# Gram products of two head pairs in one block, and the recurrence's first sums directly behind the solve

## The chip, the cores and the metric

The kernel runs on one core of a Trainium2 chip. The metric is the device time of one execution in microseconds, as the median of several runs; lower is better.

## What is computed

The reference is a trunk of two layers on a sequence of 512 tokens with 1024 channels. Each layer normalizes its input, projects it with one wide matrix, runs three mixers side by side on the columns (an RWKV-7 recurrence, a chunked retention, a gated spatial mixing), merges them through sigmoid gates, and adds a gated MLP with a short convolution. Cut to its frame:

```python
for l in range(DEPTH):
    h = rmsnorm(x, norm1_g[l])
    p = h @ w_in[l]
    p_rw, p_ret, p_sg, gate_logits = jnp.split(p, in_cuts, axis=-1)
    y_rw = rwkv7_branch(p_rw, ...)          # 8 heads of 64 channels
    y_ret, y_sg = retention_branch(p_ret, cos, sin), sgu_branch(p_sg, ...)
    gates = jax.nn.sigmoid(gate_logits.reshape(B, S, N_BRANCH, D_MODEL))
    x = x + jnp.sum(gates * proj, axis=2) @ w_out[l]
    x = x + conv_ffn(rmsnorm(x, norm2_g[l]), ...)
return rmsnorm(x, final_g)
```

The change lies in the RWKV-7 branch, whose core is a recurrence over tokens:

```python
sa = jnp.einsum('bhvk,bhk->bhv', state, -kk_t)
state = state * w_t[:, :, None, :] + sa[..., None] * (kk_t * a_t)[:, :, None, :] + v_t[..., None] * k_t[:, :, None, :]
y = jnp.einsum('bhvk,bhk->bhv', state, r_t)
```

## The kernel before

All data are 32-bit floats. A large product is made of three matrix products of rounded halves (high x low, high x high, low x high; `mm3`, line 157), each 128x128 by 128x512. Weights come by DMA through the queue of SyncE, and ScalarE (line 140) and VectorE (line 141) split each block of 512 columns into its high and low half.

The recurrence is not run token by token. The 512 tokens are cut into 8 chunks of 64, and the 8 heads stand in 4 pairs `m`, one head on each half of the 128 partitions. The branch goes through these steps:

- Projections. `cols3(m)` computes the k, r and v columns of pair m (`col`, 24 dense products each), `col(13)` the columns of the output gate.
- `prep(m)` computes decay factors and the scaled operands `x` and `bk` on ScalarE and VectorE, from two small projections (lines 565 and 566). Then come its **Gram products** (lines 603 and 606): for each of two groups of four chunks, 16 products of 64x64 by 64x128 go into two PSUM tiles, `pB` and `pK`. ScalarE copies the tiles to `GB` and `Y` (lines 607 and 608), and POOL masks their upper triangles (lines 611 and 612).
- `bonus(m)` sums r times k over the channels of a head by two dense products with a block of ones (lines 620 and 621) and multiplies the sum with v.
- `vturn` and `bturn` transpose v and `bk` by way of DRAM; their DMAs stand in the queue of SyncE.
- `solve` inverts the 64x64 unit triangular matrix of each of the 64 head-chunks. Copies on ScalarE and POOL (lines 801 and 803) gather the 32x32 diagonal blocks, VectorE transposes them (line 813) and inverts them in 31 serial steps (lines 820 and 822), and after line 826 two rounds of 32x32 products join the halves (lines 841 and 850), each followed by copies out of PSUM (lines 845 and 854).
- The recurrence over the 8 chunks (products all on line 696) alternates with copies on VectorE and ScalarE. Its first products are the sums `Q` of chunk 0, from `Y` and the transposed v.

Where PE would stand still it works on **fillers**: projections that the branch doesn't need, the gates above all (`gates`, 24 column blocks of 24 products; one step of the generator, a fill, is 12 products). Before the change 36 fills stand between the last `prep` and the first 32x32 products, two between the rounds, one more and then one more ahead of `Q`, and one between the steps of each chunk.

What sets the order: the program is written as one stream of instructions, and a scheduler orders each engine's instructions ahead of time by data dependence, free buffers, program order as a priority and a simulated timeline. An instruction given to `keep_in_program_order` (`po` in the code, or `pin` in a fill) is ordered behind the instruction that the program wrote last for its engine; others may be taken between, and instructions without it may move ahead when they are ready earlier. Each engine then runs its list strictly in order.

PSUM has two pools of four tiles of 128x512: `acc` for the large products and `sm` for the small ones (`pB`, `pK`, the sums of `bonus`, the solve's tiles, `Q` and `P1`).

Of the kernel before, what the change touches and what calls it, by code (L numbers as in the profile page):

```python
# [21 lines left out]
RWC, RETC, SGC = 1792, 1536, 1024  # L22
NU, NR, NFP = 31, 16, 39
FIRST = (12, 4, 0, 8)
FILL = (36, 2, 1)
KEPT = 6
PRE = {(0, "f", 2): 0, (0, "f", 4): 1, (0, "f", 6): 2, (0, "f", 8): 3, (0, "d", 0): 4, (0, "d", 1): 5, (0, "d", 2): 6, (0, "d", 3): 7,
       (0, "d", 4): 8, (0, "d", 5): 9, (0, "d", 6): 10}
# [24 lines left out]
class Emit:  # L53
# [440 lines left out]
    def rwkv(self, l, nst):  # L494
        nc, V, A, a = self.nc, self.nc.vector, self.nc.scalar, self.a
        T, P = nc.tensor, nc.gpsimd
# [3 lines left out]
        po = self.tc.keep_in_program_order if l == 0 else lambda i: i  # L500
# [9 lines left out]
        n2, pr, sw = self.small((128, 4, 8), "n2"), self.small((128, 4, 16), "pr"), self.small((128, 4, 8), "sw")  # L510
# [11 lines left out]
        def col(m):  # L522
            ps = ready.pop(m) if m in ready else self.colF(l, m)
            p = self.r(n="rwp")
            V.tensor_tensor(p, ps, self.rsF, op=MUL)  # L525
# [7 lines left out]
        for i in range(2):  # L533
            x = self.u(n="wax")
# [23 lines left out]
        def prep(m):  # L558
# [3 lines left out]
            ms = slice(m * 128, m * 128 + 128)  # L562
# [4 lines left out]
            x, y = [self.rw((128, 8, 128), n, 4) for n in ("X", "Y")]  # L567
            bk = self.rw((128, 8, 2, 64), "bk", 4)
# [26 lines left out]
            V.tensor_tensor(bk[:, :, 1, :], q8(kp), q8(Eout), op=MUL)  # L595
            V.transpose(tha, ksq)
            V.tensor_reduce(pr[:, m], tha.rearrange("p (j r) -> p j r", r=32), axis=AX.X, op=ADD)
            for g in range(2):
                pB, pK = [self.sm((128, 4, 128)) for _ in range(2)]
                for j in range(4):  # L600
                    c = 4 * g + j
                    for h in range(2):
                        i = T.matmul(pK[hv[1 - h], j, :], bk[hv[h], c, 1, :], x[hv[h], c, :], start=True, stop=True)  # L603
                        if c or h:
                            po(i)
                        po(T.matmul(pB[hv[h], j, :], bk[hv[h], c, 0, :], x[hv[h], c, :], start=True, stop=True))
                A.copy(GB[:, 8 * m + 4 * g:8 * m + 4 * g + 4, :], pB)
                A.copy(y[:, 4 * g:4 * g + 4, :], pK)
            for h in range(2):
                yr, gr = y[hv[h]].rearrange("p c (a t) -> p c a t", a=2), GB[hv[h], 8 * m:8 * m + 8, 64:128]  # L610
                P.affine_select(yr, yr, [[0, 8], [1, 2], [1, 64]], ALU.is_ge, 0.0, base=-1, channel_multiplier=-1)
                P.affine_select(gr, gr, [[0, 8], [1, 64]], ALU.is_ge, 0.0, base=0, channel_multiplier=-1)
            X.append(x); Y.append(y); BK.append(bk)

        def bonus(m):
            kp, r, v = kc[m], rc[m], Vf[m]
            V.scalar_tensor_tensor(kp, r, self.p("rk", m), kp, op0=MUL, op1=MUL)
            kh, kl = self.split(kp, self.r)
            pbn = self.sm()
            po(T.matmul(pbn, self.bonesR, kl, start=True, stop=False))  # L620
# [15 lines left out]
        prep(1)  # L636
        cols3(3)
        bonus(1)
        prep(2)
        gd = col(13)  # L640
        bonus(2)
        prep(3)
        bonus(3)
        A.activation(gd, gd, AF.Tanh, scale=0.5)
        V.tensor_scalar(gd, gd, 0.5, 0.5, op0=MUL, op1=ADD)
# [24 lines left out]
        vop = lambda R, m, c: Vf[m][R].rearrange("p (e c d) -> p e c d", e=2, d=32)[:, :, c, :]  # L670
# [8 lines left out]
        n2 = n2.rearrange("p m c -> p (m c)")  # L679
# [5 lines left out]
            for m in range(4):  # L685
                bturn(m, 0)

        self.solve(GB, n2, turns)

        yT, mh = [], [(m, h) for m in range(4) for h in range(2)]

        def mm(o, l, r, start=False):
            po(T.matmul(o, l, r, start=start, stop=True, skip_group_check=True))  # L696

        while back:
            po(A.copy(*back.pop(0)))
        self.fill(1, True)  # L700
        self.fill(FILL[2], True)
        Q = self.sm((128, 2, 4, 64))
        for m, h in mh:
            mm(Q[hv[h], 1, m, :], Y[m][hv[1 - h], 0, 0:64], vop(hv[1 - h], m, 0), m == 0)
        for c in range(8):
            if c % 2 == 0:
                y = self.r(n="y")
# [77 lines left out]
            self.yrw.append(self.split(t, self.f))  # L785
            yield

    def solve(self, G, n2, then):


        V, A, T = self.nc.vector, self.nc.scalar, self.nc.tensor
# [56 lines left out]
        for g, i in [(g, i) for g in range(2) for i in range(16)]:  # L848
            for h in range(2):
                po(T.matmul(pt[g][h][(lo, hi)[i % 2][h], i, :], zs[g][hi[h], i, :], TT[hi[h], 16 * g + i, :], start=True, stop=True))  # L850
# [631 lines left out]
```

## Time and profile before

| what | value |
|---|---|
| median of 3 runs | 1690.54 us (1690.29 to 1692.25) |
| span of the profiled execution | 1688.8 us; no other time of that execution is given |
| PE (TensorE) busy | 1680.2 us, 99% |
| VectorE, ScalarE, POOL busy | 1217.9, 793.7, 261.3 us |
| granted TensorE clock | 1.000 over the span |
| Gram products, layers 0 and 1 | from 64.86 to 124.56 and from 898.33 to 975.40 us |
| solve's first product | at 197.59 and 1041.62 us |

A row of the timeline gives the start in microseconds from the beginning of the span, the duration, the engine, the line of the kernel, what is written and read, shapes and a count. Dense products overlap, so PE's progress is read from the distance of starts. Each of the small 32-bit products stands in the profile as two rows. A wait is written as the engine, line and tile that waited, the releaser behind an arrow, and the idle time.

### The profile page before, as it was taken

Reading aid. Unit: us, or ns where it says so; the run is one execution under the profiler, and the core shown is the slowest. Engines: PE = TensorE matmul, PEld = TensorE weight load, DVE = VectorE, ACT = ScalarE, POOL = GpSimd, SP = SyncE. Lnnn points to the kernel's source line nnn. Section 1 sums busy time; section 2 is a strip of 40 time slices with the busy share of each in tenths; the row PEclk is TensorE's granted clock in tenths of the full one; section 3 lists DMA queues with packets and bytes.
Section 4 is the critical chain, followed back from the end, with each engine's and each line's share of the span. In section 5 each row is a group of like instructions: output and inputs, shape, how many; then the busy total and the mean of one; then the engine's idle time right before and its main releaser. Section 6 shows DMA issues by size and latency. Waiting matters only on the chain.

```text
span 1688.8 us, 27952 instructions
## 1 busy us (share of the span) xinstructions
PE 1680.2 (99%) x10247; PEld 1381.5 (82%) x10247; DVE 1217.9 (72%) x2115; ACT 793.7 (47%) x1365; POOL 261.3 (15%) x376
## 2 busy tenths in 40 slices
PE   9999999999999999999999999999999999999998
PEld 7888877888888888888888888778888888888887
DVE  7887746578669877655568888465786688887877
ACT  6563433554255444433346544335542544444565
POOL 1121000312301200003321210003122012220000
PEclk9999999999999999999999999999999999999999
DMA  5236563634544533247743366536344434443775
GB/s 183 88 109 199 176 187 95 184 122 134 191 144 148 195 122 97 63 146 261 252 145 99 94 207 184 174 101 188 118 137 163 154 96 144 142 141 110 244 248 177
DMA packets 143385, 260.01 MB, mean 154 GB/s; under 512 B 19440, under 2 KB 35440, under 8 KB 143248
## 3 DMA queue, kind: packets, MB, share of 16 engines
q1 hardware_dynamic: 117056, 188.41, 35.9%
q0 software_dynamic: 17552, 54.15, 9.8%
q10 hardware_dynamic: 8640, 15.67, 2.6%
q8 instruction: 80, 1.31, 0.3%
q14 instruction: 57, 0.47, 0.1%
HBM read 212.94 MB, written 45.22 MB: 153 GB/s over the span
## 4 chain that ended last, share of the span: by engine, by line
PE 97%; DVE 1%; DMA 1%; issue 0%; ACT 0%; SPq 0%; ACTq 0%; DVEq 0%
PE acc L157 88%; PE sm L157 3%; PE sm L696 2%; PE sm L948 1%; PE sm L603 1%; PE sm L1059 0%; DMA wr<-wall 0%; DMA tr<-bkT 0%; DVE wl L141 0%; PE acc L359 0%; PE sm L566 0%; PE sm L565 0%; PE sm L1006 0%; PE sm L850 0%; PE acc L319 0%
## 5 line engine op out<-in xcount | busy, mean ns | idle before, releaser
L157 PE MATMUL acc<-lo,sh 128*128 128x512 f32 x1108 | 432.0, 390 | 0.0
L157 PE MATMUL acc<-hi,sh 128*128 128x512 f32 x1108 | 431.4, 389 | 0.0
L157 PE MATMUL acc<-hi,sl 128*128 128x512 f32 x1108 | 424.6, 389 | 0.0
L140 ACT CAST sh<-wr 128x512 fp32r<-128x512 f32 (+1 forms) x375 | 226.8, 614 | 309.1 <-PE acc L157 165.6
L141 DVE TENSOR_TENSOR sl<-wr,sh 128x512 fp32r<-128x512 f32 (+1 forms) x375 | 252.0, 680 | 94.9 <-ACT sh L140 78.9
L141 DVE TENSOR_TENSOR wl<-wr,wh 128x512 fp32r<-128x512 f32 x238 | 169.0, 713 | 139.4 <-ACT wh L140 133.6
L140 ACT CAST wh<-wr 128x512 fp32r<-128x512 f32 x238 | 146.8, 619 | 242.8 <-PE acc L157 154.6
L157 PEld LDWEIGHTS acc<-lo,sh 128*128 128x128 f32 x1108 | 208.0, 188 | 43.8 <-issue 0.3
L157 PEld LDWEIGHTS acc<-hi,sl 128*128 128x128 f32 x1108 | 208.0, 188 | 43.1 <-issue 0.2
L157 PEld LDWEIGHTS acc<-hi,sh 128*128 128x128 f32 x1108 | 208.0, 188 | 43.0
L157 PE MATMUL acc<-lo,wh 128*128 128x512 f32 x584 | 230.0, 394 | 0.4 <-DVE rwp L525 0.4
L157 PE MATMUL acc<-hi,wl 128*128 128x512 f32 x584 | 228.3, 391 | 0.1
L157 PE MATMUL acc<-hi,wh 128*128 128x512 f32 x584 | 227.6, 390 | 0.0
L1125 ACT ACTIVATE cv<-fu,pc 128x512 f32<-128x512 f32 x88 | 71.7, 816 | 138.4 <-DVE fu L1123 138.4
L157 PEld LDWEIGHTS acc<-hi,wl 128*128 128x128 f32 x584 | 109.6, 188 | 24.6 <-issue 0.9
L157 PEld LDWEIGHTS acc<-lo,wh 128*128 128x128 f32 x584 | 109.6, 188 | 24.2 <-DVE rwp L525 0.8
L157 PEld LDWEIGHTS acc<-hi,wh 128*128 128x128 f32 x584 | 109.7, 188 | 22.3 <-issue 0.2
L157 PE MATMUL acc<-ah,sh 128*128 128x512 f32 x352 | 108.4, 389 | 0.0
L1126 DVE SCALAR_TENSOR_TENSOR cv<-fu,pc,cv 128x511 f32<-128x511 f32 x88 | 65.8, 749 | 34.5 <-ACT cv L1125 34.4
L157 PE MATMUL acc<-wl,hi 128*128 128x512 f32 x212 | 85.7, 404 | 0.0
L1123 DVE TENSOR_TENSOR fu<-acc,rsF 128x512 f32<-128x512 f32 x88 | 60.3, 685 | 30.8 <-PE acc L157 29.8
L157 PE MATMUL acc<-wh,hi 128*128 128x512 f32 x212 | 82.5, 389 | 0.0
(368 smaller groups left out, 2447.5 us busy)
## 6 DMA issues: line engine op xcount, KB each, us to landing
wr<-wall SPq DMA_DIRECT2D x480, 256.0 KB, 2.9
gd<-gth ACTq DMA_DIRECT2D x48, 256.0 KB, 3.4
gth<-gd POOLq DMA_DIRECT2D x48, 256.0 KB, 3.7
pre<-wdt POOLq DMA_DIRECT2D x44, 256.0 KB, 6.1
ts<-pre POOLq DMA_DIRECT2D x44, 256.0 KB, 2.8
wr<-ts SPq DMA_DIRECT2D x44, 256.0 KB, 4.1
wr<-wdn SPq DMA_DIRECT2D x40, 256.0 KB, 4.3
wr<-wdt SPq DMA_DIRECT2D x33, 256.0 KB, 4.1
```

Source lines behind the costliest of these rows:

```text
L140: self.kept(self.nc.scalar.copy(hi[:, :n], raw[:, :n]))
L141: self.kept(self.nc.vector.tensor_tensor(lo[:, :n], raw[:, :n], hi[:, :n], op=SUB))
L157: i = self.nc.tensor.matmul(*x, **y, **kw)
L603: i = T.matmul(pK[hv[1 - h], j, :], bk[hv[h], c, 1, :], x[hv[h], c, :], start=True, stop=True)
L696: po(T.matmul(o, l, r, start=start, stop=True, skip_group_check=True))
L948: po(T.matmul(o, lhsT, rhs, start=start, stop=stop, skip_group_check=True))
L1123: V.tensor_tensor(u, ps, self.rsF, op=MUL)
L1125: A.activation(t, u, AF.Identity, scale=self.p("cw2", j), bias=self.p("cb", j))
L1126: V.scalar_tensor_tensor(t[:, 1:], u[:, :511], self.p("cw1", j), t[:, 1:], op0=MUL, op1=ADD)
```

## The change

`prep(m)` ends before its Gram products. They move to a new function `gram(ms)`, which writes them for two pairs, four groups one behind the other, with all products in program order. The two PSUM tiles of the third group are taken from the pool `acc`; those of the other three come from `sm`. The masks of POOL for both pairs follow behind the products of both.

The calls become: projections of all pairs and of the output gate ahead of `prep(2)`; `gram((1, 0))` behind `prep(2)`; 6 fills; `bonus(2)` and `prep(3)`; 6 fills; `gram((3, 2))`; `bonus(3)`. The fills between this point and the solve's first products go from 36 to 24, so their sum stays.

The sums `Q` of chunk 0 become a function `begin`, which `solve` calls between its second round of products and the copies of their result. `Q` now takes a tile of `acc`. The two fills that stood ahead of the sums now follow them.

```diff
-FILL = (36, 2, 1)
+FILL = (24, 2, 1)
+GRAM = (6, 6)
...
-            for g in range(2):
-                pB, pK = [self.sm((128, 4, 128)) for _ in range(2)]
+            X.append(x); Y.append(y); BK.append(bk)
+
+        def gram(ms):
+
+            for m, g in [(m, g) for m in ms for g in range(2)]:
+                x, y, bk = X[m], Y[m], BK[m]
+                pB, pK = [(self.acc if (m, g) == (ms[1], 0) else self.sm)((128, 4, 128)) for _ in range(2)]
                 for j in range(4):
                     c = 4 * g + j
                     for h in range(2):
-                        i = T.matmul(pK[hv[1 - h], j, :], bk[hv[h], c, 1, :], x[hv[h], c, :], start=True, stop=True)
-                        if c or h:
-                            po(i)
+                        po(T.matmul(pK[hv[1 - h], j, :], bk[hv[h], c, 1, :], x[hv[h], c, :], start=True, stop=True))
                         po(T.matmul(pB[hv[h], j, :], bk[hv[h], c, 0, :], x[hv[h], c, :], start=True, stop=True))
                 A.copy(GB[:, 8 * m + 4 * g:8 * m + 4 * g + 4, :], pB)
                 A.copy(y[:, 4 * g:4 * g + 4, :], pK)
-            for h in range(2):
+            for m, h in [(m, h) for m in ms for h in range(2)]:
...
         bonus(1)
+        gd = col(13)
         prep(2)
-        gd = col(13)
+        gram((1, 0))
+        self.pool = None
+        self.fill(GRAM[0])
         bonus(2)
         prep(3)
+        self.fill(GRAM[1])
+        gram((3, 2))
         bonus(3)
...
-        self.solve(GB, n2, turns)
+        def begin():
+
+            q = self.acc((128, 2, 4, 64))
+            for m, h in mh:
+                mm(q[hv[h], 1, m, :], Y[m][hv[1 - h], 0, 0:64], vop(hv[1 - h], m, 0), m == 0)
+            return q
+
+        Q = self.solve(GB, n2, turns, begin)
         while back:
             po(A.copy(*back.pop(0)))
         self.fill(1, True)
         self.fill(FILL[2], True)
-        Q = self.sm((128, 2, 4, 64))
-        for m, h in mh:
-            mm(Q[hv[h], 1, m, :], Y[m][hv[1 - h], 0, 0:64], vop(hv[1 - h], m, 0), m == 0)
...
                 po(T.matmul(pt[g][h][(lo, hi)[i % 2][h], i, :], zs[g][hi[h], i, :], TT[hi[h], 16 * g + i, :], start=True, stop=True))
+        q = begin()
         for g in range(2):
             for h in range(2):
                 for e in range(2):
                     (V.tensor_copy if h else A.copy)(G[lo[h], 16 * g + e:16 * g + 16:2, 32:64], pt[g][h][(lo, hi)[e][h], e::2])
+        return q
```

More of the change, by code (lines that the diff above doesn't have):

```diff
@@ L608, in prep @@
                 A.copy(y[:, 4 * g:4 * g + 4, :], pK)
-            for h in range(2):
-                yr, gr = y[hv[h]].rearrange("p c (a t) -> p c a t", a=2), GB[hv[h], 8 * m:8 * m + 8, 64:128]
+            for m, h in [(m, h) for m in ms for h in range(2)]:
+                yr, gr = Y[m][hv[h]].rearrange("p c (a t) -> p c a t", a=2), GB[hv[h], 8 * m:8 * m + 8, 64:128]
                 P.affine_select(yr, yr, [[0, 8], [1, 2], [1, 64]], ALU.is_ge, 0.0, base=-1, channel_multiplier=-1)
                 P.affine_select(gr, gr, [[0, 8], [1, 64]], ALU.is_ge, 0.0, base=0, channel_multiplier=-1)
-            X.append(x); Y.append(y); BK.append(bk)
         def bonus(m):
@@ L786, in rwkv_out, with solve @@
             yield
-    def solve(self, G, n2, then):
+    def solve(self, G, n2, then, begin):
         V, A, T = self.nc.vector, self.nc.scalar, self.nc.tensor
```

## The prediction

> **What bounds the kernel now.** I read the page first: the busy line and the chain that ended last.
>
> ```profile
> span 1688.8 us, 27952 instructions
> PE 1680.2 (99%) x10247; PEld 1381.5 (82%) x10247; DVE 1217.9 (72%) x2115; ACT 793.7 (47%) x1365; POOL 261.3 (15%) x376
> PE 97%; DVE 1%; DMA 1%; issue 0%; ACT 0%; SPq 0%; ACTq 0%; DVEq 0%
> ```
>
> PE is never without work, so a time is what PE issues plus what it waits. Next the list of waits of PE, all of it:
>
> ```profile
> PE acc L359 <- DVE rst L356: 1.5, 1, 1.5
> PE sm L620 <- ACT Y L608: 0.5, 1, 0.5
> PE sm L696 <- DVE s L756: 0.4, 2, 0.2
> PE acc L157 <- DVE rwp L525: 0.4, 1, 0.4
> ```
>
> That is 2.8 us, 1.5 of it at the very start. No wait stands at the Gram products (L603, L606) or at the solve (L841, L850). What is left to gain at these places is what PE loses when it goes from dense products to small ones and back, inside "busy". The chain in order of time shows dense stretches of three lengths (start, us, what):
>
> ```profile
> 8.44 13.60 PE acc L157 x60
> 198.92 5.67 PE acc L157 x24
> 212.25 2.95 PE acc L157 x12
> ```
>
> 60 in 13.60 us are 0.2267 us each. 24 of them should take 5.44 and 12 of them 2.72; both stretches take 0.23 more, whatever their length. The timeline of PE over the first Gram block of layer 0 shows where (start, duration; a duration is a product's latency, so I use differences of starts):
>
> ```profile
> 64.54 0.39 PE L157 MATMUL acc<-lo,wh 128*128 128x512 f32 x1
> 64.86 0.32 PE L603 MATMUL sm<-X,bk 64*64 64x128 f32 x1
> ...
> 65.02 0.27 PE L603 MATMUL sm<-X,bk 64*64 64x128 f32 x1
> ...
> 66.55 0.27 PE L603 MATMUL sm<-X,bk 64*64 64x128 f32 x1
> ...
> 66.77 0.50 PE L157 MATMUL acc<-hi,wh 128*128 128x512 f32 x1
> 67.11 0.40 PE L157 MATMUL acc<-hi,wl 128*128 128x512 f32 x1
> ...
> 67.58 0.40 PE L157 MATMUL acc<-hi,wh 128*128 128x512 f32 x1
> 68.43 0.50 PE L620 MATMUL sm<-lo,bonesR 128*128 128x512 f32 x1 [0.45 <-ACT Y L608]
> ```
>
> The 64 rows of a block are 32 products, two rows each, and start four at a time. From 65.02 to 66.55 fourteen fours pass, 0.109 us each; sixteen should take 1.75. The block takes 66.77 - 64.86 = 1.91, so 0.16 more. The way in is 0.32 instead of 0.227 (0.09 more), and the three dense steps after it take 0.81 instead of 0.68 (0.13 more). **One excursion from dense work to small work and back costs 0.38 us**, beside the small products themselves. The dense side of it, 0.09 + 0.13, is the 0.23 of the stretches above.
>
> **The change part by part.** No product is added or taken away: 432 fill products a layer stay 432 (36 fills of 12; after it 6 + 6 + 24), and the vector, scalar and POOL work of prep and solve keeps its instructions. What changes is the number of excursions, and who waits.
>
> *Gram in two blocks a layer instead of four.* Two excursions less a layer, four in the program: 4 x 0.38 = **-1.5 us**. Nothing hides it, since it lies on PE.
>
> *The first sums behind the solve's second product.* Before, 24 fill products separate the two:
>
> ```profile
> 204.52 1.46 PE L850 MATMUL sm<-cs,zs 32*32 32x32 f32 x128
> ...
> 211.57 0.68 PE L696 MATMUL sm<-Vt,Y 64*64 64x64 f32 x16
> 212.18 0.50 PE L157 MATMUL acc<-lo,wh 128*128 128x512 f32 x1
> ```
>
> Joined, the dense side's 0.23 is gone. But the products here go from tiles of 32x32 to tiles of 64x64, and no row of this trace shows that step. At best it costs nothing, and the narrow side's 0.16 is saved too (0.39 a layer); at worst it costs as much as the dense side (0 a layer). I take 0.2, in the middle, because every change of shape that has a row here costs something: **-0.4 us** for two layers, bounds 0 and -0.8. The Trainium skill (TensorEngine Tiling (Array Packing), Key Properties) says that changing the tiling mode, not just the tile, drains the engine; a 32x32 to 64x64 step is such a change. By that rule the join keeps a drain, and the sum would be at the 0 end, 0.4 us later than mine; the rows above agree with it as far as they go (dense to 64x64 is paid for both ways). The sums come out in a slot of the other PSUM pool and are held until the copy of L719; the fills need one slot of four in turn, so three serve them. What the sums no longer cover, the copies of the solve's result, still has three fills ahead of the first product that needs it: 36 x 0.2267 = 8.2 us against 24 before and 12 behind the sums, the same.
>
> *A wait that loses its cause.* The row of 68.43 above is the bonus product of pair 0: it needs a PSUM slot which the Gram copies on ACT hold. From 67.58 to 68.43 are 0.85 instead of 0.23, and the waits' view names it. After the change pair 0's and pair 1's bonus come ahead of any Gram product. **-0.6 us**, bounds 0 (it comes back at pair 3's bonus, which stands directly behind the second block) and -0.6.
>
> *A wait that gets a cause.* A merged block has four groups of two PSUM tiles. Three take slots of the small pool, which has four, and one takes the other pool's; so the fourth group needs the slots of the first, and starts at 3 x 0.875 = 2.63 us into the block (a group is eight fours of 0.109). They are free when ACT has made two copies. In layer 0's last block and in layer 1's first block (starts on PE, then ACT):
>
> ```profile
> 122.65 0.32 PE L603 MATMUL sm<-X,bk 64*64 64x128 f32 x1
> 123.81 0.59 ACT L608 COPY Y<-sm 128x512 f32<-128x512 f32 x1 [1.44 <-PE sm L606]
> 124.29 0.59 ACT L607 COPY GB<-sm 128x512 f32<-128x512 f32 x1
> ```
> ```profile
> 898.33 0.29 PE L603 MATMUL sm<-X,bk 64*64 64x128 f32 x1
> 904.15 0.62 ACT L140 CAST sh<-wr 128x512 fp32r<-128x512 f32 x1 [5.25 <-DMA wr<-wall]
> 906.80 0.58 ACT L607 COPY GB<-sm 128x512 f32<-128x512 f32 x1
> ```
>
> The first has its second copy done 2.23 us into the block (124.88): no wait, 0.4 to spare. In the second ACT sits in its order behind a cast whose weights are late, and is done at 9.05: PE would stand 6.4 us, and all dense work with it. Bounds 0 and 6.4 a block. The new blocks stand where the projections are over and fills run, like the first row, so I take 0.1 a block: **+0.4 us** over four. The Trainium skill (the same page, PSUM Bottleneck) says that tiling speeds up TensorE but not the emptying of PSUM; the copies, 0.48 us apart, against a group of two tiles in 0.875 bear it out. By that rule alone a block would go at ACT's pace, 4 x 0.96 instead of 4 x 0.875, and four blocks would cost 1.4 us instead of my 0.4: the first rival below.
>
> *The solve's cover.* The solve's serial chain (POOL copies, DVE steps) runs under the fills between the last Gram product and L841, and the products behind it are pinned, so lateness there is PE idle, one for one. Rows of POOL, DVE and PE:
>
> ```profile
> 125.44 2.37 POOL L611 TENSOR_SCALAR_AFFINE_SELECT Y<-Y 64x1024 f32<-64x1024 f32 x2 [14.26 <-ACT Y L608]
> 127.87 1.71 POOL L612 TENSOR_SCALAR_AFFINE_SELECT GB<-GB 64x512 f32<-64x512 f32 x2
> 129.53 2.60 POOL L803 COPY cs<-GB 32x1024 f32<-32x1024 f32 x2
> ```
> ```profile
> 136.78 0.69 DVE L141 TENSOR_TENSOR wl<-wr,wh 128x512 fp32r<-128x512 f32 x1 [3.75 <-ACT wh L140]
> ...
> 138.01 2.06 DVE L813 STREAM_TRANSPOSE cs<-cs 128x1024 f32<-128x1024 f32 x1
> ...
> 185.65 2.31 DVE L826 STREAM_TRANSPOSE cs<-cs 128x512 f32<-128x512 f32 x2
> ```
> ```profile
> 124.56 0.50 PE L157 MATMUL acc<-hi,wl 128*128 128x512 f32 x1
> ...
> 197.59 1.34 PE L841 MATMUL sm<-cs,GB 32*32 32x32 f32 x128
> ```
> ```profile
> 1034.02 2.27 DVE L826 STREAM_TRANSPOSE cs<-cs 128x512 f32<-128x512 f32 x2
> ```
> ```profile
> 975.40 0.50 PE L157 MATMUL acc<-hi,wl 128*128 128x512 f32 x1
> ...
> 1041.62 1.34 PE L841 MATMUL sm<-cs,GB 32*32 32x32 f32 x128
> ```
>
> Before, the chain is done 63.4 us after the last Gram product in layer 0 (187.96 - 124.56) and 60.9 in layer 1; L841 comes at 73.0 and 66.2. Afterwards the second block is ordered behind 12 fills, so 24 fills and the bonus remain: 288 x 0.2267 + 0.46 + 0.23 = 66.0 in both. The chain's head grows: POOL now masks two pairs behind one block (another 2.37 + 1.71), but starts on the first of them 1.75 earlier, so its copy is done 2.3 later. Before, POOL's copy was done at 132.13 and DVE took it up at 138.01, behind a wait for weights; if this 5.9 us swallows the 2.3, there are 2.6 us to spare in layer 0 and 5.1 in layer 1, and if not, 0.3 and 2.8. Either way **0**.
>
> **Sum:** -1.5 - 0.4 - 0.6 + 0.4 = -2.1 us on a span of 1688.8, so 1686.7. The page gives no other time of that execution; the median of the runs, 1690.54, lies 1.7 above its span, and I keep that: **1688.4 us**.
>
> **The rivals.**
>
> *Block held up or split.* Pins here give an order, not a neighbourhood, and the fills are not pinned: where the order is planned with the fourth group waiting, a fill slips in, and the excursion is back (0.38), or PE waits about as much. For it: the four slots are the pool's whole size. Against it: 2.23 against 2.63. All four blocks: -2.5 + 4 x 0.4 = -0.9, **1689.6 us**.
>
> *The solve comes late* (slower). Place: L841, both layers. If a wait for weights like the 3.75 of 136.78 falls behind L813 rather than ahead of it, where POOL's 2.3 can't hide: layer 0 63.4 + 2.3 + 3.75 = 69.4 against 66.0, 3.4 late; layer 1 66.9, 0.9 late. -2.1 + 4.3 = +2.2, **1692.7 us**. It decides once the chain ends over 66.0 us behind the block, and loses over 0.2% when the two layers are 5.5 late together. Against it: the four transposes of v and the sums of squares, which DVE did behind the last Gram block, can now be done ahead of it.
>
> *ACT blocked under one merged block* (slower): the 6.4 us of layer 1's row once, -2.5 + 6.4 = +3.9, **1694.4 us**. Against it: it takes a late weight just there.
>
> *More than excursions.* The best end of each term, -1.5 - 0.8 - 0.6, and the two listed waits of 0.4 gone as well by a new order: -3.7, **1686.8 us**. Against it: nothing in the diff touches L756 or L525.
>
> **How the numbers follow.** A measurement of this kernel tells about 0.2% from no change, 3.4 us: below 1687.2 is faster, above 1693.9 slower. Forecast 0.53, from 1687.6 to 1689.5 by its own bounds; held up or split 0.16; solve late 0.10; ACT blocked 0.06; more than excursions 0.15. The first two are no change, and most of the third. Faster gets the last case and a little of the forecast's lower edge, 0.19; slower the blocked case and the tail of the late solve, 0.11; the same 0.70. The range is from 1686.7 (the best end) to 1692.7 (the solve late), leaving out the blocked case and what no row shows.
>
> **What would show it.** Right: two blocks of 128 Gram rows a layer with no L157 row inside, each about 2 x 1.75 + 0.16 = 3.7 us long; 36 dense products in one stretch behind L696's first sums, at 8.4 us; no wait of PE at L620; L841 without idle ahead of it. Wrong: PE rows with idle at L603 or L606 released by ACT L607 or L608 (held up), at L841 released by DVE L826 (solve late), or dense stretches elsewhere that are broken more often than before.

## The result, and the profile after

The changed kernel is **slower**: 1701.79 us median (1699.13 to 1703.63) against 1690.32, ratio 1.0064 (95% interval 1.0052 to 1.0076). The forecast of 1688.4 was on the wrong side of no change, and the range ended at 1692.7; a slower kernel had been given a chance of 0.11. The profiled execution of the changed kernel took 1701.35 us, with a span of 1699.6; of before it was 1688.8. Lines after the edit are 1 to 10 higher: the dense product L157 is now L158, the Gram products L603 and L606 are L609 and L610, ACT's copies behind them L611 and L612, the solve's products L849 and L858, the recurrence's L699.

The page of the changed kernel: span, busy line, and the chain that ended last by engine and by line.

```profile
span 1699.6 us, 27942 instructions
PE 1685.2 (99%) x10247; PEld 1382.6 (81%) x10247; DVE 1220.5 (72%) x2115; ACT 793.2 (47%) x1365; POOL 260.2 (15%) x376
PE 89%; issue 4%; DVE 3%; DMA 2%; ACT 1%; SPq 0%; POOL 0%; ACTq 0%; DVEq 0%; POOLq 0%
PE acc L158 81%; PE sm L158 3%; PE sm L699 2%; PE sm L958 1%; DMA tr<-vT 0%; DMA wr<-wall 0%; DVE wl L142 0%; SPq L661 0%; PE sm L1069 0%; ACT wh L141 0%; DMA tr<-bkT 0%; PE acc L360 0%; PE sm L1016 0%; DVE X L590 0%; ACT GB L611 0%
```

PE still reads 99% busy. What changed is the chain: before, 97% of it was PE; now it leaves PE for 11% of the span, and weight loads (wr), round trips of the turned v (tr<-vT), casts (wh, wl) and Gram copies (GB) stand in it. The waits of PE, the longest (us in total, times, longest):

```profile
PE acc L158 <- ACT wh L141: 2.7, 6, 1.2
...
PE acc L158 <- DVE wl L142: 1.4, 2, 0.7
PE acc L158 <- DVE rwp L526: 1.3, 1, 1.3
PE sm L609 <- ACT Y L612: 0.7, 2, 0.3
```

Three rows are new: dense fillers that wait for the weights' high part (L141) and low part (L142), and Gram products that wait for a slot (L612). The row of L526 stood there before with 0.4. The bonus wait at L620, now L623, is gone, as forecast. A wait costs more than its idle time (around the 0.71 us of idle at 103.74, shown below, the starts fall behind by 0.99 us), so I compare starts. The windows view gives busy time by stretch (start and end; length; busy us and instructions of PE, PEld, DVE, ACT, POOL; PE's granted clock; DMA share; GB/s): of the kernel before from the last Gram product of layer 0 to the solve, then of the changed kernel over the first block, between the blocks and from the second block to the solve, in layer 0, and the last of these in layer 1.

```profile
124.60:197.60 73.00, 72.94 (x325) 59.40 (x321) 58.21 (x119) 29.26 (x46) 10.23 (x10) 1.00 0.63 195
```
```profile
88.30:93.70 5.40, 4.86 (x130) 3.86 (x129) 3.99 (x8) 5.23 (x10) 0.00 (x0) 1.00 0.10 36
93.70:129.30 35.60, 34.73 (x153) 27.92 (x150) 29.34 (x51) 19.32 (x37) 9.71 (x8) 1.00 0.38 117
...
133.40:202.30 68.90, 67.17 (x293) 53.88 (x290) 53.63 (x110) 26.25 (x42) 12.72 (x13) 1.00 0.57 183
...
983.30:1052.00 68.70, 67.91 (x293) 53.59 (x290) 53.80 (x110) 25.73 (x41) 12.84 (x14) 1.00 0.56 186
```

So PE now idles 0.5 us inside the first block, 0.9 between the blocks, and 1.7 and 0.8 behind the second block, where the fillers are to cover the solve and where 0.1 was idle before. By differences of starts, from the first product of the preparation to the solve's first product (and from there to the second group of the recurrence's sums):

| stretch | before | after | difference |
|---|---|---|---|
| start to the first L565/L566 of layer 0 | 45.95 | 46.61 | +0.7 |
| layer 0, to the solve | 151.63 | 155.75 | +4.1 |
| of it from Gram product to Gram product | 7.63 | 9.30 | +1.7 |
| layer 0, solve to the second group of sums | 17.55 | 17.90 | +0.35 |
| layer 1, to the solve | 158.42 | 163.75 | +5.3 |
| of it from Gram product to Gram product | 7.63 | 9.30 | +1.7 |
| layer 1, solve to the second group of sums | 17.55 | 17.77 | +0.2 |

The sum is +10.7 of the span's +10.8; everything else takes as long as before. The +0.7 at the start lies ahead of the branch's preparation. Over all the kernels below this first stretch takes 45.2 to 46.8 us, with the wait at L526 in it at up to 1.3 us; why it varies is open. Three other things are to be explained: Gram rows that should have got shorter and got longer, dense work that got longer by 2.4 and 3.7, and a join that costs.

**The Gram block.** PE, then ACT, over the first block of layer 0 (start, duration):

```profile
88.40 0.32 PE L609 MATMUL sm<-X,bk 64*64 64x128 f32 x1
...
89.33 0.39 PE L609 MATMUL sm<-X,bk 64*64 64x128 f32 x2
...
92.17 0.43 PE L609 MATMUL sm<-X,bk 64*64 64x128 f32 x2 [0.33 <-ACT Y L612]
...
93.69 0.50 PE L158 MATMUL acc<-lo,wh 128*128 128x512 f32 x1
```
```profile
88.57 0.67 ACT L576 ACTIVATE cs<-sm,haw 128x512 f32<-128x512 f32 x1
89.14 0.68 ACT L588 ACTIVATE cs<-sm,haw 128x512 f32<-128x512 f32 x1
...
91.55 0.57 ACT L612 COPY Y<-sm 128x512 f32<-128x512 f32 x1
92.01 0.59 ACT L611 COPY GB<-sm 128x512 f32<-128x512 f32 x1
```

The block takes 5.3 us, not 3.7. Its second group stops at 89.33, until ACT has read the two sums of the third preparation (L576, L588), whose products were issued directly ahead of the block and which hold two of the four slots. Its fourth group waits for the first two copies, which ACT makes only at 91.55 and 92.01, behind activations of the third preparation and of the output gate. The second block of the layer, 129.35 to 133.37, takes 4.0.

One rule fits 35 of the 36 merged blocks in the traces here, those of the experiments included: from the end of the second copy to the block's end it is 1.08 us. In these two blocks the copy ends 4.20 and 2.94 us in, and they take 5.28 and 4.02. (The 36th has no wait and takes 3.65.) The stop at 89.33 therefore costs nothing of its own: the later wait covers it.

**The fillers.** SP's DMA queue behind the second block, before (upper) and after:

```profile
131.78 1.04 SPq L127 DMA_DIRECT2D wr<-wall  x2
134.10 1.74 SPq L653 DMA_DIRECT2D Vt<-tr  x4
135.88 0.42 SPq L243 DMA_DIRECT2D tr<-vT  x1
136.40 0.38 SPq L127 DMA_DIRECT2D wr<-wall  x1
```
```profile
131.14 0.36 SPq L128 DMA_DIRECT2D wr<-wall  x1
131.54 2.29 SPq L661 DMA_DIRECT2D Vt<-tr  x2
133.87 0.42 SPq L244 DMA_DIRECT2D tr<-vT  x1
136.43 1.71 SPq L661 DMA_DIRECT2D Vt<-tr  x4
...
144.39 0.30 SPq L661 DMA_DIRECT2D Vt<-tr  x1
144.79 0.38 SPq L128 DMA_DIRECT2D wr<-wall  x1
```

A round trip writes the turned tile out (tr<-vT) and reads it back (Vt<-tr); the read waits in SP's order for the write to land, and what is queued behind it waits too (between 128 and 150 us four such reads wait 6.7 us in all). Before, weight loads stood between the trips, and the longest time from one load's issue to the next was 8.6 us here (123.21 to 131.78); now it is 13.7 us (131.14 to 144.79; the rows left out belong to the trips). A tile of weights serves 12 dense products, 2.72 us at 0.2267 each. Ten microseconds after the gap PE stands:

```profile
154.33 0.50 PE L158 MATMUL acc<-lo,wh 128*128 128x512 f32 x1 [1.17 <-ACT wh L141]
```

The load for this tile went out at 147.23 and landed at 151.57. The cast takes 0.62 us, and PE's last product ended at 153.16, so this was in time. But the cast had to wait on ACT (SP's rows, then ACT's):

```profile
147.23 0.38 SPq L128 DMA_DIRECT2D wr<-wall  x1
...
151.03 1.26 SPq L661 DMA_DIRECT2D bkS<-tr  x3
```
```profile
149.12 0.63 ACT L478 ACTIVATE gth<-gth 128x512 f32<-128x512 f32 x1
153.20 0.36 ACTq L480 DMA_DIRECT2D gd<-gth  x1
153.66 0.62 ACT L141 CAST wh<-wr 128x512 fp32r<-128x512 f32 x1 [3.91 <-PE acc L158]
```

Ahead of the cast stands L480, the issue of the DMA that writes a finished gate to DRAM. The trace keeps the semaphore of every wait. The wait instruction ahead of this issue ends at 153.16, 0.04 us after a read of a trip (bkS<-tr, issued at 151.40) landed, and that read signals the same semaphore as the gate's write behind it. All 30 waits of this kind in the trace are for the semaphore that the issue itself then signals, so I take it that an issue waits until the transfer that last used its semaphore has landed. (PE, which the row of the cast names, is the profile's inference.) The kernel before has 34 such waits; the longest leaves ACT idle for 2.6 us, against 4.2 now. So the trips make weights late in two ways: by their place in SP's queue, and by ACT's wait for them. Behind the second blocks PE waits five times for a cast. Two of the five, 1.17 and 0.41 us, are of the second kind, with the weights landed 2.1 and 1.9 us ahead of the cast. In the other three, 0.57, 0.18 and 0.20 us, the weights landed 0.1 us ahead of the cast.

The stretch between the blocks has another cause. There PE, ACT and DVE show

```profile
103.74 0.50 PE L158 MATMUL acc<-hi,wl 128*128 128x512 f32 x1 [0.71 <-DVE wl L142]
```
```profile
101.11 0.62 ACT L150 CAST hi<-rwc 128x512 fp32r<-128x512 f32 x1 [1.47 <-DVE rwc L620]
101.63 1.13 ACT L141 CAST wh<-wr 128x512 fp32r<-128x512 f32 x2
```
```profile
102.56 1.13 DVE L142 TENSOR_TENSOR wl<-wr,wh 128x512 fp32r<-128x512 f32 x1
```

The weights have landed (at 83.7 and 86.8), but their cast stands on ACT behind pair 2's bonus cast, which waits for DVE, and their split on DVE behind that bonus: 1.4 us a layer, the restart of the products included.

**The join.** The timeline of PE over the first sums, then the wait instructions at the recurrence's line around them, after and before (count, duration in ns, first and last start):

```profile
210.71 1.20 PE L699 MATMUL acc<-Vt,Y 64*64 64x64 f32 x16
211.84 0.50 PE L158 MATMUL acc<-lo,wh 128*128 128x512 f32 x1
```
```profile
L699 PEldq EVENT_SEMAPHORE  x8: 51/51/51, 210.5 to 211.4; - x8
```
```profile
L696 PEldq EVENT_SEMAPHORE  x10: 51/51/51, 207.4 to 211.9; - x10
```

The eight products (16 rows) wait for many tiles, and each has a wait instruction of its own on PE's queue of weight loads. Before, nine of the ten waits were worked off from 207.4 to 210.6 while the fillers ran, and the 16 rows then took 0.61 us (211.57 to 212.18). Joined, they lie between the products, eight in 0.9 us, and the rows take 1.13 us (210.71 to 211.84): the weight loads of a product now come every 0.125 us, where before they came every 0.058. Over eight products this is 0.54 us, all of the 0.52 that the rows got longer; less the dense side's 0.23 it leaves the 0.2 to 0.35 of the table. The 36 dense products behind them ran as forecast, in 8.4 us.

### The profile page after: what moved, and what is told of

Its sections match the earlier page's. It is cut to its first block, busy times and chain, and to the rows that moved or that the text cites. A ratio compares the mean times of both kernels' runs of the same rounds, so it can differ in the third digit from the quotient of the medians.

```text
span 1699.6 us, 27942 instructions
## 1 busy us (share of the span) xinstructions
PE 1685.2 (99%) x10247; PEld 1382.6 (81%) x10247; DVE 1220.5 (72%) x2115; ACT 793.2 (47%) x1365; POOL 260.2 (15%) x376
## 4 chain that ended last, share of the span: by engine, by line
PE 89%; issue 4%; DVE 3%; DMA 2%; ACT 1%; SPq 0%; POOL 0%; ACTq 0%; DVEq 0%; POOLq 0%
PE acc L158 81%; PE sm L158 3%; PE sm L699 2%; PE sm L958 1%; DMA tr<-vT 0%; DMA wr<-wall 0%; DVE wl L142 0%; SPq L661 0%; PE sm L1069 0%; ACT wh L141 0%; DMA tr<-bkT 0%; PE acc L360 0%; PE sm L1016 0%; DVE X L590 0%; ACT GB L611 0%
## 5 line engine op out<-in xcount | busy, mean ns | idle before, releaser
L158 PE MATMUL acc<-lo,sh 128*128 128x512 f32 x1108 | 432.0, 390 | 0.0
L158 PE MATMUL acc<-hi,sh 128*128 128x512 f32 x1108 | 431.4, 389 | 0.0
L158 PE MATMUL acc<-hi,sl 128*128 128x512 f32 x1108 | 424.5, 389 | 0.0
L141 ACT CAST sh<-wr 128x512 fp32r<-128x512 f32 (+1 forms) x375 | 226.7, 614 | 304.8 <-PE acc L158 169.6
L142 DVE TENSOR_TENSOR sl<-wr,sh 128x512 fp32r<-128x512 f32 (+1 forms) x375 | 252.6, 682 | 97.1 <-ACT sh L141 72.6
L142 DVE TENSOR_TENSOR wl<-wr,wh 128x512 fp32r<-128x512 f32 x238 | 168.2, 711 | 149.8 <-ACT wh L141 149.0
L141 ACT CAST wh<-wr 128x512 fp32r<-128x512 f32 x238 | 146.7, 619 | 247.2 <-PE acc L158 172.3
L158 PEld LDWEIGHTS acc<-lo,sh 128*128 128x128 f32 x1108 | 208.0, 188 | 43.5 <-issue 0.3
L158 PEld LDWEIGHTS acc<-hi,sl 128*128 128x128 f32 x1108 | 208.0, 188 | 43.5
L158 PEld LDWEIGHTS acc<-hi,sh 128*128 128x128 f32 x1108 | 208.0, 188 | 42.6
L158 PE MATMUL acc<-lo,wh 128*128 128x512 f32 x584 | 230.8, 395 | 4.1 <-ACT wh L141 2.7
L158 PE MATMUL acc<-hi,wl 128*128 128x512 f32 x584 | 228.6, 391 | 1.4 <-DVE wl L142 1.4
L158 PE MATMUL acc<-hi,wh 128*128 128x512 f32 x584 | 227.7, 390 | 0.0
L158 PEld LDWEIGHTS acc<-lo,wh 128*128 128x128 f32 x584 | 109.6, 188 | 30.7 <-ACT wh L141 5.8
L158 PEld LDWEIGHTS acc<-hi,wl 128*128 128x128 f32 x584 | 109.6, 188 | 28.3 <-DVE wl L142 5.4
L158 PEld LDWEIGHTS acc<-hi,wh 128*128 128x128 f32 x584 | 109.7, 188 | 22.1
L158 PE MATMUL acc<-ah,sh 128*128 128x512 f32 x352 | 108.3, 389 | 0.0
L158 PE MATMUL acc<-wl,hi 128*128 128x512 f32 x212 | 85.7, 404 | 0.0
L158 PE MATMUL acc<-wh,lo 128*128 128x512 f32 x212 | 82.5, 389 | 0.0
L158 PE MATMUL acc<-wh,hi 128*128 128x512 f32 x212 | 82.4, 389 | 0.0
```

The source lines that it names most:

```text
L141: self.kept(self.nc.scalar.copy(hi[:, :n], raw[:, :n]))
L142: self.kept(self.nc.vector.tensor_tensor(lo[:, :n], raw[:, :n], hi[:, :n], op=SUB))
L158: i = self.nc.tensor.matmul(*x, **y, **kw)
```

## The experiments

**Each part alone.** `q_only` is the kernel before with the join alone; `gram_only` is the changed kernel without it, the sums again behind the two fills and in the small pool (its edit against the changed kernel):

```diff
-            q = self.acc((128, 2, 4, 64))
+            q = self.sm((128, 2, 4, 64))
...
-        Q = self.solve(GB, n2, turns, begin)
+        self.solve(GB, n2, turns, lambda: None)
...
+        Q = begin()
```

> The kernel before with one part of the change: the first sums joined directly behind the solve's second product, Gram products and fillers as before. Theory L (the loss is late operands at PE: late weights during the solve, a Gram block held up by PSUM slots, and sums joined too early): the joined sums took 1.13 us in the profile after (210.71 to 211.84) against 0.61 before, so this alone costs 0.2 to 0.4 us a layer, +0.4 to +0.8 us over the kernel before. The forecast's own step: -0.4 us (bounds 0 to -0.8). Rival J (the joining causes most of the loss): +5 to +11 us.

> The changed kernel with the first sums put back behind the two fillers in the pool they had before; merged Gram products and hand-set fillers stay. Theory L: all of the loss but the join's stays, +9 to +11 us over the kernel before, 0.4 to 0.8 us under the changed one. Rival J (the joining causes most): within 1 us of the kernel before. The forecast: -1.7 us.

Measured: `q_only` 1.0004 (0.9995 to 1.0013), no difference that can be measured; `gram_only` 1.0070 (1.0055 to 1.0085). In the trace of `q_only` the solve to the second group of sums takes 0.35 and 0.28 us longer than before: the join costs 0.6 us and earns nothing, but the loss is not in it. `gram_only` was expected a little under the changed kernel and is not under it; the intervals overlap. In its trace the trips on SP happened to leave an even longer stretch without a load (131.8 to 146.2), and PE's longest wait for weights is 2.2 us against 1.2 (again behind L480: these weights had landed 2.1 us ahead of their cast).

**The order of the fillers alone.** `fills_only` keeps the Gram products pair by pair:

```diff
-FILL = (36, 2, 1)
+FILL = (24, 2, 1)
+GRAM = (6, 6)
...
-        prep(2)
         gd = col(13)
+        prep(2)
+        self.pool = None
+        self.fill(GRAM[0])
         bonus(2)
         prep(3)
+        self.fill(GRAM[1])
```

> The kernel before with its Gram products still pair by pair in the preparation, but with col(13) ahead of the third preparation and fillers set by hand, 6 behind it, 6 behind the fourth and 24 behind the solve's start, as in the changed kernel. Theory L, in the form that the hand-set order of fillers makes the weight loads late (the turned v's round trips on SP's queue stand together while 36 fillers run without a break): +4 to +8 us over the kernel before. Rival M (it takes the merged Gram products): within 1 us of the kernel before.

Measured: 1.0032 (1.0020 to 1.0043), 5.4 us. So the merged products aren't needed for part of the loss. It lies in layer 0 alone: 157.24 us to the solve against 151.63, while layer 1 has 158.38 against 158.42. PE has one wait of 2.1 us for weights there, ending at 157.59; their load was issued at 153.03, behind trips, and landed at 156.27. Behind the wait come 3.1 us at about half the granted clock (PE's clock is the first number behind POOL's):

```profile
159.70:162.80 3.10, 3.10 (x9) 2.37 (x9) 3.00 (x8) 1.25 (x2) 0.00 (x0) 0.53 0.51 113
```

By an estimate from this row (3.1 us at 0.53) the clock costs some 1.5 of the 5.6 us of layer 0.

**SP's queue.** `v_pool` moves the four round trips of the turned v from SP's to POOL's queue; PE's order stays. `b_v_pool` does the same in the kernel before.

```diff
-            turn(o, self.trip(t, nc.sync), lambda h: 1 - h)
+            turn(o, self.trip(t, nc.gpsimd), lambda h: 1 - h, nc.gpsimd)
```

> The kernel gram_only with the four round trips of the turned v issued on POOL's DMA queue and not on SP's; PE's order is the same. Theory L puts 2.4 us in layer 0 and 1.4 us in layer 1 down to fillers whose weights SP's queue brings late because these trips stand ahead of their loads: 3 to 4.5 us less than gram_only. Rival B (the weights are late because the DMA engines or the casts on ACT and VectorE are late): within 0.7 us of gram_only.

> Control: the kernel before with the edit of v_pool (the four round trips of the turned v on POOL's queue). Theory L: the kernel before has only 0.3 us of late weights in the solve to gain, and the recurrence's late copies that v_pool shows (1.6 us and 0.6 us in layer 0, 1.7 in layer 1) may come with POOL's trips: -0.5 to +4 us against the kernel before. Rival G (POOL's queue gains in any kernel): 3 us or more under it.

Measured: `v_pool` 1.0039 (1.0026 to 1.0052), 5 us under `gram_only`; `b_v_pool` 0.9994 (0.9985 to 1.0004), no gain. SP's queue in `v_pool`, and its windows from the second block to the solve, both layers:

```profile
126.09 23.14 SPq L128 DMA_DIRECT2D wr<-wall  x8
```
```profile
133.40:199.30 65.90, 65.90 (x293) 54.33 (x290) 52.96 (x109) 25.31 (x41) 20.11 (x27) 1.00 0.63 196
982.20:1048.30 66.10, 66.07 (x297) 54.38 (x294) 52.55 (x109) 25.52 (x41) 20.09 (x27) 1.00 0.62 196
```

Eight loads go out one behind the other, and PE idles for 0.03 us at most in the 66 us that the forecast had for this cover. That the trips on SP's queue make the fillers starve is shown: the two covers are 10.1 us shorter than in `gram_only` (65.96 and 66.06 us against 71.07 and 71.06 by starts), of which the two recurrences lose 4.3 again. How much of it is SP's order and how much ACT's wait at L480 this edit can't tell, since it takes the trips out of the way of both. The kernel before, whose loads kept their places between the trips, has nothing to gain.

`v_early` leaves the trips on SP's queue and issues each behind its own pair's bonus; `b_v_early` is the control.

```diff
         bonus(1)
+        vturn(1)
...
-        for m in range(4):
-            vturn(m)
```

> The kernel gram_only with one edit: each round trip of a turned v is issued directly behind that pair's bonus and not in one row of four behind the last one, on SP's queue as before. Theory L: the fillers behind the solve's start find their weights, the waits of PE for weights between the last Gram product and the solve's first product go (3.0 us in layer 0 and 2.4 us in layer 1 of the profile of gram_only), and the time is 4 to 6 us under gram_only. Rival B (the weights are late for another reason, and v_pool gained by what it took off SP's queue for good): within 1.5 us of gram_only.

> Control: the kernel before with the same edit as v_early. Theory L: the kernel before loses next to nothing to late weights in the solve (0.3 us in its profile), so the edit leaves it within 1 us. Rival G (early trips gain in any kernel, so v_early shows nothing on the change): 3 us or more under the kernel before.

Measured: `v_early` 1.0083 (1.0066 to 1.0100), no better than `gram_only`; `b_v_early` 0.9995 (0.9986 to 1.0004). The time that was expected failed, but its mechanism did not. The covers behind the second block are 3.2 and 1.8 us shorter than in `gram_only` (67.83 and 69.24), 5.0 in all, and PE's waits for weights there fall from 3.4 and 1.9 to 0.6 and 1.2 us. They don't vanish: the round trips of the solve's other operand (tr<-bkT) moved up into the place that fell free, so that from 130.6 to 144.0 there is again no load. What ate the gain lies between the blocks of layer 1, which are 5.2 us further apart (40.87 against 35.67). ACT shows there

```profile
950.16 0.62 ACT L150 CAST hi<-rwc 128x512 fp32r<-128x512 f32 x1 [2.87 <-DVE rwc L620]
```

and the cast of the next weights stands behind it at 950.69, though their load was issued at 925.54. PE waits 2.2 us for this cast and, two products later, 1.0 us for the split; then follow 5.4 us at half the clock, 2.7 us by an estimate from this row:

```profile
953.60:959.00 5.40, 5.40 (x14) 4.15 (x14) 2.51 (x5) 2.28 (x4) 0.00 (x0) 0.50 0.78 229
```

Why the bonus comes later in this run is open. So trips that are issued early do help the fillers behind the second block, and this run's time doesn't speak against the account of the trips. A trip issued early has a price on SP, too: its write waits at the head of the queue for VectorE to turn the tile (34.3 us over six waits in the whole trace, the longest 13.6).

**The block's place and its copies.** `gram_ahead` is `gram_only` with the first block ahead of the third preparation; `copies` has besides half of the copies on VectorE; `fix` joins the edits of `gram_ahead` and `v_early`.

```diff
-        prep(2)
         gram((1, 0))
+        prep(2)
```
```diff
-                A.copy(y[:, 4 * g:4 * g + 4, :], pK)
+                V.tensor_copy(y[:, 4 * g:4 * g + 4, :], pK)
```

> The kernel gram_only with one edit: the first Gram block stands ahead of the third preparation and no longer directly behind that preparation's first two products. Theory L: the block takes 5.3 us in place of 3.7 because its second and fourth groups wait for PSUM slots that ACT frees late, ACT being busy with the third preparation; ahead of it the block takes 3.7 us in both layers, and the time is 2.5 to 3.5 us under gram_only (ratio to the kernel before about 1.005). Rival P (a block of four groups waits for slots wherever it stands): the block still takes 5 us and more, the time within 0.7 us of gram_only.

> The kernel gram_only with the edits of gram_ahead and v_early together. Theory L: what is left over the kernel before is the first fillers behind the first block that wait for casts (1.2 us a layer, 2.4 in all) less the excursions saved (1.5) and the bonus wait (0.6): -1 to +2 us against the kernel before. If late weights and slots are not the whole cause, it stays 4 us or more slower.

> The kernel gram_ahead with one edit: of the two copies behind each group of Gram products the second (into Y) is made by VectorE and not by ACT. Theory L: in gram_ahead each block of 3.65 us still takes 4.6, since the fourth group waits for PSUM slots until ACT has made its eight copies one by one; with two engines the blocks take 3.7 to 4.0 us, and the Gram rows sum to 7.3 to 8.0 us a layer in place of 9.2: 2 to 4 us under gram_ahead. Rival D (VectorE, 72% busy, brings the copies and what stands behind them as late): blocks of 4.5 us and more, the time within 1 us of gram_ahead or over it.

Measured: `gram_ahead` 1.0040 (1.0025 to 1.0055), 5 us under `gram_only`, more than expected; yet the block still takes 4.65 us (87.40 to 92.05) where 3.7 was expected, and the second one 4.57. The gain came from elsewhere: the casts between the blocks were in time, and the fillers waited less behind the second. On the block rival P was nearer: the second group's wait went, the fourth's stayed. In `gram_ahead` ACT comes to the copies only when it is through with activations that stand ahead of them in its order and wait for DVE:

```profile
89.38 0.63 ACT L652 ACTIVATE rwc<-rwc 128x512 f32<-128x512 f32 x1 [0.82 <-DVE rwc L529]
...
90.38 0.59 ACT L611 COPY GB<-sm 128x512 f32<-128x512 f32 x1
```

The second copy is done at 90.97, 3.57 us into the block; the fourth group is due at 2.63. In `fix` one block shows the other case, the first of layer 1:

```profile
933.13 0.32 PE L609 MATMUL sm<-X,bk 64*64 64x128 f32 x1
...
936.78 0.50 PE L566 MATMUL sm<-lo,wus 128*128 128x512 f32 x1
```
```profile
934.28 0.58 ACT L612 COPY Y<-sm 128x512 f32<-128x512 f32 x1 [3.16 <-PE sm L610]
934.76 0.59 ACT L611 COPY GB<-sm 128x512 f32<-128x512 f32 x1
```

Here the copies are done 2.22 us in, and the block takes 3.65. So the time of a block hangs on when ACT is free for its first two copies (1.08 us from the second one's end, here as in the changed kernel), and a block without a wait is as long as forecast. `copies` gave 1.0043 (1.0026 to 1.0059), no better than `gram_ahead` although the Gram rows fell from 9.2 to 8.5 us a layer; half of what was expected of the blocks, and lost again behind late casts in the solve of layer 0 and late copies in its recurrence (2.5 us there). The Trainium skill (TensorEngine Tiling (Array Packing), PSUM Bottleneck) advises to empty PSUM with both engines; the blocks' 9.2 to 8.5 agrees, the whole time doesn't show it. `fix` gave 1.0024 (1.0014 to 1.0033), 4.1 us slower than before, against an expected -1 to +2 and a rival with 4 or more: late weights and slots as they were understood there are not the whole cause.

**All causes at once.** `fix2` is `gram_ahead` with the trips on POOL's queue, `fix3` the same with the copies shared.

> The kernel gram_ahead with the edit of v_pool: first Gram block ahead of the third preparation, the turned v's round trips on POOL's queue. Theory L: of the 6.3 us that gram_ahead lies over the kernel before, the late weights in the solve go (2.2 us in layer 0 and 0.9 in layer 1 of its profile), the blocks held by PSUM slots stay (9.2 us a layer against 7.6): 2 to 4 us slower than the kernel before, more by what POOL's trips cost in the recurrence. If the weights are late for another reason it stays with gram_ahead, 6 us slower.

> The kernel fix2 with the copies of the Gram products shared between ACT and VectorE as in copies: all the causes named so far taken away at once. Theory L: what is left is the saving of two excursions a layer (1.5 us) and of the bonus wait (0.5) against what POOL's trips cost (0 to 4): -2 to +2 us against the kernel before. If a cause is still unnamed it stays 4 us or more slower.

Measured: `fix2` 1.0036 (1.0025 to 1.0047); `fix3` 1.0018 (1.0008 to 1.0027), 3 us slower than the kernel before. By its time `fix2` stands at its rival's number (6 us), not at the 2 to 4 that were expected; but its weights come in time, so the rival's reason is not the one. It shows another loss:

```profile
199.33 0.85 PE L850 MATMUL sm<-cs,GB 32*32 32x32 f32 x78 [1.53 <-DVE cs L835]
```

The solve is late, at 67.6 us behind the second block (131.76) where the cover is 66. The trips on POOL are the likely cause: POOL's copies for the solve are done 14.6 and 15.8 us behind the blocks, against 10.0 in `gram_ahead`, whose serial chain of the solve is through in 64.55 and 64.35. `fix3` was expected at -2 to +2 and lies a little above. It has no wait at the solve, and up to the solve it stands at 150.76 and 158.93 us against 151.63 and 158.42 before: the causes named account for the loss in these stretches. What keeps it slower is in the recurrence, 1.3 and 1.9 us longer than before:

```profile
PE sm L699 <- ACT U L742: 2.0, 2, 1.3
```

Waits of this kind, for ACT's or DVE's part of the recurrence, show in the traces of `v_pool`, `copies`, `fix2` and `fix3` and once in `q_only` (0.4 us or less in `fills_only`, `fix` and `b_v_early`), not in those of the changed kernel, `gram_only` or `b_v_pool`. What holds ACT is the issue L480 once more: in all six waits for the copy U in `v_pool`, `copies` and `fix3`, the copy, or a cast ahead of it, stands behind L480, whose wait ends 0.03 to 0.04 us after a transfer of SP's queue landed that signals its semaphore. For the 1.3 us above this is a load of weights, issued at 226.88 and landed at 230.51. Why it falls so in these versions and not in the others is open. No version here beats the kernel before.

All kernels side by side; the stretch runs from the preparation's first product to the solve's first, Gram rows are the part of it from Gram product to Gram product:

| kernel | ratio to before | stretch, layer 0 and 1 | Gram rows in each |
|---|---|---|---|
| before | 1 | 151.63, 158.42 | 7.63, 7.63 |
| after | 1.0064 | 155.75, 163.75 | 9.30, 9.30 |
| `q_only` | 1.0004 | 151.97, 158.75 | 7.63, 7.63 |
| `gram_only` | 1.0070 | 157.84, 166.02 | 9.30, 9.32 |
| `fills_only` | 1.0032 | 157.24, 158.38 | 7.63, 7.63 |
| `v_pool` | 1.0039 | 152.73, 161.21 | 9.30, 8.81 |
| `v_early` | 1.0083 | 154.62, 168.67 | 8.92, 8.56 |
| `gram_ahead` | 1.0040 | 154.49, 162.59 | 9.23, 9.24 |
| `fix` | 1.0024 | 152.96, 159.96 | 8.94, 8.32 |
| `copies` | 1.0043 | 155.19, 160.91 | 8.52, 8.45 |
| `fix2` | 1.0036 | 152.83, 160.65 | 9.22, 9.22 |
| `fix3` | 1.0018 | 150.76, 158.93 | 8.45, 8.46 |
| `b_v_pool` (control) | 0.9994 | 150.93, 159.16 | 7.63, 7.63 |
| `b_v_early` (control) | 0.9995 | 151.07, 158.35 | 7.63, 7.63 |

## Why the prediction was wrong, step by step

*The excursions, -1.5.* Right as far as it goes. Two blocks before take 2 x 1.91 us, and one merged block without a wait takes 3.65 (`fix`); the dense side's 0.23 is then paid once and not twice. 3.82 + 0.23 - 3.65 is 0.40 saved, 0.38 forecast.

*The join, -0.4.* The sign was wrong: +0.57 after, +0.63 in `q_only`. The step looked at what a change of tile shape costs. What decides is that PE's wait instructions for these 16 rows had been hidden under 24 dense products, and joining took their cover away. My best end, 0.8 saved, and my worst, 0, were both on the wrong side. The drain that the prediction takes from the Trainium skill (TensorEngine Tiling (Array Packing), Key Properties) would by its working have left the join at 0. The shape changes once here, but all eight products come at 0.125 us with a wait ahead of each, and that pace accounts for the difference without a drain.

*The bonus wait, -0.6.* Right: no wait at L623 in either layer. Before, it cost 0.7 by starts.

*The fourth group, +0.4.* Too small by a factor of ten: the four blocks took 1.6, 0.4, 1.6 and 0.4 us over 3.65, 4.0 in all. The mechanism stood in the sum with its bounds, 0 to 6.4 a block. The failed step is "the new blocks stand where the projections are over and fills run, like the first row, so I take 0.1 a block". The first block stands directly behind the third preparation's products, and six activations, four of that preparation and two of the output gate, run on ACT ahead of the first copy. The diff shows the place.

*The solve's cover, 0.* Right, and for the reason given. The chain is through (the last transposes, now L834) 63.1 and 62.8 us behind the block, inside the 66.0; the forecast had 63.4 to 65.7 in layer 0 and 60.9 to 63.2 in layer 1. POOL's copy is done 2.4 us later than before, 2.3 forecast, and DVE takes it up 3.4 us after that, behind a wait for weights (both in layer 0). That the margin is small, as the rival with the late solve had it, shows with the trips on POOL's queue: it shrinks to 0.5 and 0.1 us (`v_pool`), or the solve is 1.5 late (`fix2`).

*What wasn't in the sum at all* was the largest part. "432 fill products a layer stay 432" counted PE's work only. Moving 12 fillers ahead moved the weight loads against eight round trips on SP's queue and the casts against ACT's waits for those trips, and put other casts behind a bonus on ACT and VectorE. The late weights cost some 5 us in the two solves and 2.8 between the blocks (waits and the restarts behind them, by starts); with 4.0 in the blocks, 0.6 at the join and 0.7 at the start, less 1.6 and 0.7 saved and 0.5 that the kernel before lost to late weights, that is the +10.7 of the table within 0.4. Neither of the two slower rivals named it: both spoke of a late weight only as something that delays DVE or ACT, not as what PE itself waits for. Two of the prediction's signs of being wrong did come: Gram products that wait for ACT's copies, and dense stretches that are broken more often. (The lower end of the range is given as 1686.7 and its case as 1686.8; nothing hangs on it.)

## What to carry to other kernels

A filler is a load, a cast, a split and a product; whoever moves it by hand moves a place in each of four queues, and the queue that works in order with round trips in it is the one to cost first. A DMA that a compute engine issues is a wait in that engine's order, too: ask which transfer it waits for, and what stands behind it. Before joining small products to what is ahead of them, look at what their waits were hidden under. A block that gathers groups needs the engine that empties PSUM to be free at its start, so read that engine's order around the new place, not around the old one.

## What the hardware showed unexpectedly

After a wait of PE of 2 to 3 us the granted clock can fall to half: 0.53 for 3.1 us in `fills_only` behind a wait of 2.1 us, 0.50 for 5.4 us in `v_early` behind waits of 2.2 and 1.0 us, and a dense product every 0.427 us there instead of 0.227. In `gram_only` a wait of 2.2 us had no such end: its clock stays at 1.00 in the window after it. The Trainium skill (TensorE: Matmul & The Clock Gate, Part 1: The HAM clock gate) gives an idle window of about 3.4 us, running freely, as what throttles; that the same wait does it in one run and not in another fits a free-running window, while a single wait of 2.1 us is shorter than that figure. A product's wait instruction has a price of its own on PE, seen only where nothing runs ahead of it: eight products of 64x64 (16 rows) took 1.13 us with eight such waits between them, and 0.61 with the waits worked off before. And the issue of a DMA on ACT can wait for a transfer of SP's queue that signals the same semaphore: 13 of the 30 waits ahead of gate writes in the changed kernel leave ACT idle for 0.3 us or more, 4.2 at most, each until such a transfer has landed.
